# A two-layer encoder trunk: group A's attention in paired matmuls, an early activation table, the norm inside the MLP's squares, and another order of projections

## The chip, the core and the metric

The kernel runs on one core of one Trainium2 chip. The time is device microseconds of one execution. TensorE multiplies (a weight load, then columns that stream past it), VectorE and ScalarE do elementwise work and empty PSUM, GpSimd does memsets and some DMA, SyncE issues DMA. Each engine takes its own instructions strictly in order and they meet through semaphores.

## The reference

`x` is 512 tokens by 1024 features, and there are two layers. In each:

```
xn = RMSNorm(x)
[A | B | C | gates] = xn @ W_in            # 7296 columns
A: 3 groups x 2 heads of 64: windowed softmax attention, dilations 1, 4, 16;
   the groups are weighted by their softmax denominators
B: 4 heads: difference of two softmax maps, per-head RMSNorm
C: 4 heads: retention, both directions; per-head RMSNorm, times silu(cg)
m  = sum_i sigmoid(gate_i) * (branch_i @ W_branch_i)      # i = A, B, C
x  = x + m @ W_o
x  = x + relu(RMSNorm(x) @ W_1)^2 @ W_2                    # 4096 wide
```

All of it is float32. The kernel splits each operand into a rounded high part and the remainder (`hi`, `lo`) and multiplies hi\*hi + hi\*lo + lo\*hi, three matmuls for one product.

## The kernel before

Tokens are ordered so that a query tile of 128 rows (four tiles, index `j`) holds one residue class modulo 4. For dilations 4 and 16 (groups g = 1, 2) a tile then attends to itself alone (the "diagonal" groups); for dilation 1 (g = 0) all tiles meet (the "dense" group).

The work is a list of chunks, `sequence` (L822), each one `gemm` (L287): for pairs of 128 input rows ("units") a weight block is fetched by SyncE (`raw`), split by ScalarE and VectorE (`whi`, `wlo`, L282 and L283) and multiplied into four PSUM banks `acc0` to `acc3`. After the last unit, `done` empties each bank. The chunks A, B and C ("waves") make q, k and v of a group or a head. G makes 512 gate columns, W an output product with a branch's weights times its gate, cg the silu gate of C, O the product with W_o, M1 and M2 the two halves of the MLP, a quarter at a time. A wave has 96 matmuls of 384 columns (C: of 512), G 96 of 512.

The attention itself runs beside the chunks as "side" threads: `thread_prep` (norm, rope, transposes into `qk`), `thread_a`, `thread_b`, `thread_c`. `build` (L1022) interleaves their steps with the chunk's, by a table of costs per engine; a chunk can say that it needs a flag (W of A needs all of A's outputs, `("y", l, 0)`), and side steps then go on alone. `emit` (L1054) at last puts all instructions into one queue per engine, with the same costs, earliest start first. So an edit that alters a cost moves instructions on every engine. Side work uses four PSUM banks (`ps`), 55 SBUF tiles of 2 KB a partition (`U`) and two `qk` tiles.

`qk` holds q, then k's high part and a third slot that pairs q's remainder with k, so that a score takes two matmuls (`score`, L524). In `prep` (L473) the lower copy into that slot is a DVE copy (L520). For A, `vh` and `vl` are 128 wide per head with 64 columns zeroed by GpSimd (L443), so that two heads add into one bank `ps_a_tail`.

In the MLP, `norm_spread` makes `rB2`, the squared inverse norm spread over partitions. M1's `done` takes relu and squares on ScalarE without it. M2's sums over the four quarters are kept in `part` and multiplied by `rB2` at the end (L973 to L997); in the last layer the final sums go out in halves of 256 columns by DMA from SyncE and ScalarE in turn.

Of the kernel before, what the change touches and what calls it, by code (L numbers as in the profile page):

```python
# [9 lines left out]
FT = mybir.dt.float32  # L10
# [102 lines left out]
class Trunk:  # L113
# [202 lines left out]
    def setup(self):  # L316
# [90 lines left out]

    def norm_stat(self, square=False):
# [9 lines left out]
        if square:  # L418
            self.tt(r, r, r, OP.mult)
        return r  # L420
# [10 lines left out]
    def wave_buffers(self, kind):  # L431
        w = {"kind": kind}
        w["qk"] = self.take(self.qp, 2, "qk", [P, 6, SEQ], FR, "qk")
        if kind == "B":
            vt = [(self.U((P, NJ, P), FR, "vh"), self.U((P, NJ, P), FR, "vl"))]
        else:
            vt = [(self.U((P, NJ, P), FR, "vh"), self.U((P, NJ, P), FR, "vl")) for _ in range(2)]
        if kind == "A":
            for h in range(2):
                o = 64 * (1 - h)  # L440
                for t in vt[h]:
                    z = t.bitcast(FT)[:, :, o:o + 64]
                    self.op("POOL", 0.3, [t], [], lambda z=z: self.nc.gpsimd.memset(z, 0.0))  # L443
        w["v"] = vt
        w["t"] = [None, None]
        return w

    def wave_evac(self, w, j, bank):
        r = self.r[:, j:j + 1]
        if j % 2 == 0:  # L450
            w["t"][j // 2] = self.U((P, 2, 256), name="t")
        self.act(w["t"][j // 2][:, j % 2, :], bank[:, 0:256], AF.Copy, scale=r)
        for h, (vh, vl) in enumerate(w["v"]):
            if w["kind"] == "A":
                src, dst = bank[:, 256 + 64 * h:320 + 64 * h], slice(64 * h, 64 * h + 64)
            else:
                src, dst = bank[:, 256 + 128 * h:384 + 128 * h], slice(0, 128)
            self.act(vh[:, j, dst], src, AF.Copy, scale=r)
            self.stt(vl[:, j, dst], src, r, vh.bitcast(FT)[:, j, dst], OP.mult, OP.subtract)

# [12 lines left out]
    def prep(self, w, jp):  # L473
# [89 lines left out]

    def dense_out(self, w, vt, ws, av, first, last):
        for jk in range(NJ):
            hi, lo = self.to_keys(ws, jk)
            yield ("wait", "av")
            self.av_all(av, vt, jk, hi, lo, first and jk == 0, last and jk == NJ - 1)
            yield
# [59 lines left out]
    def b_tail(self, l, w, st):  # L629
        av = self.ps(name="ps_b_tail")  # L630
        yield from self.dense_out(w, w["v"][0], st["w"], av, True, True)
# [31 lines left out]
    def a_diag_scores(self, w, m, st, nmx, den, mask):  # L663
        ps = self.ps(name="ps_a_diag_scores")
        for j in range(NJ):
            self.score(w, (m,), j, (ps[:, j * P:(j + 1) * P],), n=P)
        sm = self.U(name="sm")
        s3 = sm.rearrange("p (j k) -> p j k", k=P)
        self.tt(s3, ps.rearrange("p (j k) -> p j k", k=P), mask[:, None, :].to_broadcast([P, NJ, P]), OP.add)
# [8 lines left out]
    def a_diag_out(self, w, m, st, av):  # L678
# [3 lines left out]
        hi, lo = self.split(b, "wT")  # L682
        yield ("wait", "dav")
        vh, vl = w["v"][m]
        for j in range(NJ):
            js = slice(j * P, (j + 1) * P)
            self.mm3(av[:, js], vh[:, j, :], vl[:, j, :], hi[:, js], lo[:, js], m == 0 and j == 0, m == 1 and j == NJ - 1)
        yield
# [52 lines left out]
    def a_tail(self, l, w, m, g, st, ys):  # L741
        if m == 0:
            w["av"] = self.ps(name="ps_a_tail")
        av = w["av"]
        if g == 0:
            yield from self.dense_out(w, w["v"][m], st, av, m == 0, m == 1)
        else:
            yield from self.a_diag_out(w, m, st, av)
        if m == 1:
            y = self.U(name="ya")  # L750
            self.act(y, av)
            ys.append(y)
            self.flags.add(("done", l, "A", g))
            yield

    def decay_table(self, l, h):
        T = self.take(self.Tp, 2, "T", [P, 896], FT, "T")
        dl = self.blob[:, C_DL - P:C_U - P]
        i = l * 4 + h
        self.act(T, dl, AF.Copy, scale=self.edec[:, 0, i:i + 1])  # L760
        self.stt(T, dl, self.edec[:, 1, i:i + 1], T, OP.mult, OP.min)
        self.act(T, T, AF.Exp)
        self.ts(T, T, 0.125)
        self.stt(T[:, 384:512], self.ident, 0.125, T[:, 384:512], OP.mult, OP.add)
        return T

    def c_head(self, l, w, m, h):
# [5 lines left out]
        for jk in range(NJ):  # L773
# [26 lines left out]
    def thread_prep(self, l):  # L800
        first = True
        for s in self.sequence:
# [12 lines left out]
            for jp in range(2):  # L815
# [5 lines left out]

    sequence = ([("A", 0), ("A", 1), ("A", 2), ("C", 0), ("C", 1), ("B", 0), ("B", 1), ("B", 2), ("cg",), ("G", 0, 0),  # L822
                 ("W", 0, 0), ("G", 0, 1), ("W", 0, 1), ("G", 2, 0), ("B", 3), ("W", 2, 0), ("G", 2, 1), ("W", 2, 1),
                 ("G", 1, 0), ("G", 1, 1), ("W", 1, 0), ("W", 1, 1), ("O", 0), ("O", 1)]
                + [x for i in range(4) for x in
# [24 lines left out]
    def layer(self, l, xg):  # L850
# [8 lines left out]
        h = [None] * 8  # L859
        part = {}  # L860
        self.side.append([self.thread_prep(l), None])
# [3 lines left out]
        for s in self.sequence:  # L865
# [84 lines left out]
            elif kind == "M1":  # L950
                def done(o, b):
                    t = self.U(name="rl")
                    self.act(t, b, AF.Relu)
                    hi = self.U(dt=FR, name="hh")
# [6 lines left out]
                if s[1] == 0:  # L961
                    def stat():
                        self.r2 = self.norm_stat(square=True)

# [4 lines left out]
            elif kind == "M2":  # L969
# [3 lines left out]
                def done(o, b):  # L973
                    k = s[2] * 4 + o
                    x = self.xt[k]
                    if s[1] == 0:
                        t = self.U(name="part")
                        self.act(t, b)
                        part[k] = t
                    elif s[1] < 3:  # L980
                        self.tt(part[k], part[k], b, OP.add)
                        if s[1] == 2:
                            t = part.pop(k)
                            self.tt(t, t, self.rB2, OP.mult)
                            self.tt(x, x, t, OP.add)
                    else:
                        t = self.U(name="fin")
                        self.xt[k] = None
                        for cs in ((slice(0, 256), slice(256, 512)) if last else (slice(0, 512),)):
                            self.tt(t[:, cs], b[:, cs], self.rB2[:, cs], OP.mult)  # L990
                            self.tt(x[:, cs], x[:, cs], t[:, cs], OP.add)
                            if last:
                                eng = self.nc.sync if o % 2 else self.nc.scalar
                                self.dma(eng, self.outv[k][:, cs], x[:, cs], 128, outs=[f"out{k}{cs.start}"])
                        if not last:
                            self.dma(self.nc.gpsimd, self.xspill[l + 1][k], x, 256, outs=[f"spill{l + 1}{k}"])
                            self.norm_feed(k, x)  # L997
                yield from self.gemm(c, h, done, False)
# [210 lines left out]
```

## Time and profile before

| | |
|---|---|
| runs (3) | median 1735.99 us, 1735.95 to 1737.02 |
| the profiled execution | 1736.39 us, its span 1733.8 us, granted clock 1.00 |
| TensorE busy | 1721.4 us (99%), 8232 matmuls |
| VectorE busy | 1084.2 us (63%) |
| ScalarE busy | 825.8 us (48%) |

The span is the time from the first to the last instruction of that execution. Busy matmul time is modelled at the ends, since matmuls overlap: a 512-column matmul is shown with 0.39 us, but the next one starts 0.227 us after it. What a matmul costs is therefore read from the starts of a run of them.

### The profile page before, as it was taken

The numbers are of one execution on the slowest core, as the hardware profiler recorded it, in microseconds if no ns is written. First come the engines' busy times: TensorE is split into PE (matmuls) and PEld (weight loads), VectorE is DVE, ScalarE is ACT, GpSimd is POOL, SyncE is SP. The second block draws the span as 40 slices with busy tenths as digits, with TensorE's granted clock in tenths as the row PEclk, the third lists the DMA queues.
The fourth block names the chain that finished last, engine by engine and source line by source line (L and its number), as shares of the span: only waits on it lengthen the run. The fifth ranks groups of instructions, "written<-read, shape, count | busy, mean of one in ns | idle before, by whom it ended". The sixth has DMA issues, their size and how long they took to land.

```text
span 1733.8 us, 21771 instructions
## 1 busy us (share of the span) xinstructions
PE 1721.4 (99%) x8232; PEld 1467.4 (85%) x8232; DVE 1084.2 (63%) x2123; ACT 825.8 (48%) x1514; POOL 19.5 (1%) x52
## 2 busy tenths in 40 slices
PE   8999999999999999999999999999999999999998
PEld 8889888888888888888898898888888888888887
DVE  8788998786554233344577889987766532333534
ACT  7567655554334342424456666546433453515151
POOL 0000000001000000000100000000000000000000
PEclk9999999999999999999999999999999999999999
DMA  6212222223222222222332112212232223232222
GB/s 219 100 46 71 74 67 81 72 98 122 98 97 98 97 96 95 97 97 94 107 122 80 55 62 86 73 67 92 85 122 98 98 85 110 85 110 85 98 98 73
DMA packets 48969, 160.65 MB, mean 93 GB/s; under 512 B 5728, under 2 KB 8160, under 8 KB 48736
## 3 DMA queue, kind: packets, MB, share of 16 engines
q1 hardware_dynamic: 45504, 151.84, 25.4%
q0 software_dynamic: 1920, 6.29, 1.1%
q8 instruction: 64, 1.05, 0.2%
q10 hardware_dynamic: 1440, 1.13, 0.2%
q14 instruction: 41, 0.34, 0.1%
HBM read 155.05 MB, written 4.19 MB: 92 GB/s over the span
## 4 chain that ended last, share of the span: by engine, by line
PE 97%; DVE 2%; ACT 1%; issue 0%; DMA 0%; DVEq 0%; ACTq 0%
PE acc L224 86%; PE ps_c_head L224 2%; PE ps_b_scores L224 2%; PE ps_b_tail L224 1%; PE ps_a_tail L224 1%; PE ps_to_keys L228 1%; PE ps_prep L228 1%; PE ps_a_dense_scores L224 0%; PE ps_a_diag_scores L224 0%; PE ps_yb L228 0%; PE ps_yt L228 0%; DVE wlo L185 0%; ACT vh L175 0%; ACT whi L175 0%; PE ps_a_diag_out L228 0%
## 5 line engine op out<-in xcount | busy, mean ns | idle before, releaser
L185 DVE TENSOR_TENSOR wlo<-raw,whi 128x1024 fp32r<-128x1024 f32 (+3 forms) x297 | 344.8, 1162 | 455.2 <-ACT whi L175 454.1
L175 ACT ACTIVATE whi<-raw 128x1024 fp32r<-128x1024 f32 (+3 forms) x297 | 299.9, 1010 | 631.2 <-PE acc L224 555.4
L224 PE MATMUL acc<-xgh,whi 128*128 128x512 f32 x960 | 376.5, 392 | 0.0
L224 PE MATMUL acc<-xgl,whi 128*128 128x512 f32 x960 | 374.1, 390 | 0.0
L224 PE MATMUL acc<-xgh,wlo 128*128 128x512 f32 x960 | 373.8, 390 | 0.0
L224 PEld LDWEIGHTS acc<-xgh,wlo 128*128 128x128 f32 x960 | 180.2, 188 | 37.8
L224 PEld LDWEIGHTS acc<-xgl,whi 128*128 128x128 f32 x960 | 180.3, 188 | 36.7
L224 PEld LDWEIGHTS acc<-xgh,whi 128*128 128x128 f32 x960 | 180.3, 188 | 36.7
L224 PE MATMUL acc<-whi,xgh 128*128 128x384 f32 (+1 forms) x576 | 202.4, 355 | 6.8 <-ACT whi L175 6.6
L224 PE MATMUL acc<-wlo,xgh 128*128 128x384 f32 (+1 forms) x576 | 201.2, 349 | 0.0
L224 PE MATMUL acc<-whi,xgl 128*128 128x384 f32 (+1 forms) x576 | 201.1, 349 | 0.0
L224 PE MATMUL acc<-hh,whi 128*128 128x512 f32 x512 | 199.2, 389 | 0.0
L224 PE MATMUL acc<-hl,whi 128*128 128x512 f32 x512 | 199.2, 389 | 0.0
L224 PE MATMUL acc<-hh,wlo 128*128 128x512 f32 x512 | 199.2, 389 | 0.0
L224 PEld LDWEIGHTS acc<-whi,xgh 128*128 128x128 f32 x576 | 108.4, 189 | 14.9 <-ACT whi L175 6.9
L224 PEld LDWEIGHTS acc<-wlo,xgh 128*128 128x128 f32 x576 | 108.9, 189 | 6.2 <-DVE wlo L185 0.3
L224 PEld LDWEIGHTS acc<-whi,xgl 128*128 128x128 f32 x576 | 108.6, 189 | 5.3
L224 PEld LDWEIGHTS acc<-hl,whi 128*128 128x128 f32 x512 | 96.1, 188 | 20.0
L224 PEld LDWEIGHTS acc<-hh,wlo 128*128 128x128 f32 x512 | 96.1, 188 | 19.9
L224 PEld LDWEIGHTS acc<-hh,whi 128*128 128x128 f32 x512 | 96.1, 188 | 19.9
L175 ACT ACTIVATE qk<-ps_prep 64x512 fp32r<-64x512 f32 (+1 forms) x144 | 69.9, 486 | 45.3 <-PE ps_prep L228 23.0
L185 DVE TENSOR_TENSOR hl<-rl,hh 128x512 fp32r<-128x512 f32 x64 | 44.4, 693 | 74.4 <-ACT rl L175 74.4
(202 smaller groups left out, 2285.3 us busy)
## 6 DMA issues: line engine op xcount, KB each, us to landing
raw<-in_weights_dram SPq DMA_DIRECT2D x236, 512.0 KB, 3.2
raw<-in_weights_dram SPq DMA_DIRECT2D x55, 384.0 KB, 3.0
xt<-in_x_dram SPq DMA_DIRECT2D x8, 256.0 KB, 5.8
xr<-in_x_dram POOLq DMA_DIRECT2D x8, 256.0 KB, 4.1
xspill<-xr POOLq DMA_DIRECT2D x8, 256.0 KB, 2.3
xr<-xspill POOLq DMA_DIRECT2D x8, 256.0 KB, 4.1
blob<-in_blob_dram SPq DMA_DIRECT2D x1, 1024.0 KB, 8.5
raw<-in_weights_dram SPq DMA_DIRECT2D x4, 256.0 KB, 2.6
```

What stands on the lines that cost most here:

```text
L175: lambda: self.nc.scalar.activation(out, in_, func, **k))
L185: self.dve(out, [out], [a, b], lambda: self.nc.vector.tensor_tensor(out, a, b, op=op))
L224: self.op("PE", d, [out], [lhsT, rhs], lambda: self.nc.tensor.matmul(out, lhsT, rhs, start=start, stop=stop))
L228: self.op("PE", 0.095, [out], [in_], lambda: self.nc.tensor.transpose(out, in_, ident))
```

## The change

- Group A's `v` is one tile per head: 64 columns high part, 64 columns remainder, side by side. One matmul gives both products with a given right side, in the upper and lower 64 partitions, which are then added. The GpSimd zeroing goes. Each head and, in the diagonal groups, each pair of query tiles has its own PSUM bank; ScalarE copies the upper half and VectorE adds.
- In the diagonal groups, scores and output products take both right sides (high and low) in one matmul of 256 columns instead of two or three of 128.
- A one-element `Exp` of a zeroed tile is issued at the start, so ScalarE's table load stands ahead of the first wait for data.
- `rB2` is no longer squared; M1's `done` computes max(b, 0) \* rB on VectorE and then squares. M2 adds its four quarters straight into `x`. In the last layer only the last column block goes out in halves.
- The low copy in `prep` moves from VectorE to ScalarE. In C the factor 0.125 moves from the decay table (a VectorE pass of 896 columns) into the product with the scores.
- `sequence`: G and W of branch A are put among the B waves, and cg after B2.

```diff
@@ setup
+        warm = cp.tile([P, 2], FT, name="warm")
+        self.op("POOL", 0.1, [warm], [], lambda: nc.gpsimd.memset(warm, 0.0))
+        self.act(warm[:, 1:2], warm[:, 0:1], AF.Exp)
         self.dma(nc.scalar, self.gcol, a["cols"], 18)
...
@@ wave_evac
+        if w["kind"] == "A":
+            for h, v in enumerate(w["v"]):
+                src = bank[:, 256 + 64 * h:320 + 64 * h]
+                self.act(v[:, j, 0:64], src, AF.Copy, scale=r)
+                self.stt(v[:, j, 64:128], src, r, v.bitcast(FT)[:, j, 0:64], OP.mult, OP.subtract)
+            return
...
@@ prep
-            self.copy(qk[own[m], 4 + m, qs], qk.bitcast(FT)[own[1 - m], 2 + m, qs])
+            self.act(qk[own[m], 4 + m, qs], qk.bitcast(FT)[own[1 - m], 2 + m, qs])
...
@@ dense_out
+                self.mm(av, vt[:, jk, :], hi, jk == 0, False)
+                self.mm(av, vt[:, jk, :], lo, False, jk == NJ - 1)
...
@@ a_diag_scores
-        ps = self.ps(name="ps_a_diag_scores")
-        for j in range(NJ):
-            self.score(w, (m,), j, (ps[:, j * P:(j + 1) * P],), n=P)
+        for p in range(2):
+            ps = self.ps((P, 2, 2, P), name="ps_a_diag_scores")
+            for j in range(2):
+                js = slice((2 * p + j) * P, (2 * p + j + 1) * P)
+                self.mm(ps[:, j], qk[:, m, js], qk[:, 2 + m:5 + m:2, js], j == 0, j == 1)
+            half = s3[:, 2 * p:2 * p + 2]
+            self.tt(half, ps[:, :, 0, :], mask[:, None, :].to_broadcast([P, 2, P]), OP.add)
+            self.tt(half, half, ps[:, :, 1, :], OP.add)
...
@@ a_diag_out
-            self.mm3(av[:, js], vh[:, j, :], vl[:, j, :], hi[:, js], lo[:, js], m == 0 and j == 0, m == 1 and j == NJ - 1)
+            av = self.ps((P, 2, 2, P), name="ps_a_tail")
+            for j in range(2):
+                self.mm(av[:, j], w["v"][m][:, 2 * p + j, :], ws[p][:, j], j == 0, j == 1)
+            t = self.U(name="yl")
+            t3 = t[0:64, 0:256].rearrange("p (j q) -> p j q", q=P)
+            self.act(t3, av[64:128, :, 0, :])
+            self.tt(t3, t3, av[0:64, :, 0, :], OP.add)
+            self.tt(y[own, 256 * p:256 * p + 256].rearrange("p (j q) -> p j q", q=P), t3, av[0:64, :, 1, :], OP.add)
...
@@ a_tail (dense group)
+            self.act(t[0:64], av[64:128])
+            self.tt(y[64 * m:64 * m + 64], t[0:64], av[0:64], OP.add)
...
@@ decay_table, c_head
-        self.ts(T, T, 0.125)
-            self.tt(t, ps, T[:, (3 - jk) * P:(7 - jk) * P], OP.mult)
+            self.stt(t, ps, 0.125, T[:, (3 - jk) * P:(7 - jk) * P], OP.mult, OP.mult)
...
@@ sequence
-    ("A", 0), ("A", 1), ("A", 2), ("C", 0), ("C", 1), ("B", 0), ("B", 1), ("B", 2), ("cg",), ("G", 0, 0), ("W", 0, 0), ...
+    ("A", 0), ("A", 1), ("A", 2), ("C", 0), ("C", 1), ("G", 0, 0), ("B", 0), ("B", 1), ("W", 0, 0), ("B", 2), ("G", 0, 1), ("cg",), ("W", 0, 1), ...
...
@@ M1 done
-                    self.act(t, b, AF.Relu)
+                    self.stt(t, b, 0.0, self.rB2, OP.max, OP.mult)
...
@@ M2 done
+                    if s[1] < 3:
+                        self.tt(x, x, b, OP.add)
+                        return
+                    ends = last and s[2] == 1 and o == NJ - 1
+                    for cs in ((slice(0, 256), slice(256, 512)) if ends else (slice(0, 512),)):
+                        self.tt(x[:, cs], x[:, cs], b[:, cs], OP.add)
```

The places in the queues of which the prediction speaks, where names carry the number of their buffer. First TensorE in layer 0, where a diagonal group's output product for one head (`ps_a_tail`) stands among a chunk's matmuls. Before, its first rows, the three of them coming four times:

```order
L224 MATMUL acc_340<-whi_345,xgl_140 128x512
L224 MATMUL ps_a_tail_353<-wTh_355,vh_158 128x128
L224 MATMUL ps_a_tail_353<-wTl_356,vh_158 128x128
L224 MATMUL ps_a_tail_353<-wTh_355,vl_159 128x128
L224 MATMUL ps_a_tail_353<-wTh_355,vh_158 128x128
```

and now, with the same kind of head whole:

```order
L224 MATMUL acc_364<-xgh_111,wlo_348 128x512
L224 MATMUL ps_a_tail_372<-wT_355,v_157 128x256 x2
L224 MATMUL ps_a_tail_374<-wT_356,v_157 128x256 x2
L224 MATMUL acc_365<-xgh_107,whi_347 128x512
L224 MATMUL acc_365<-xgl_108,whi_347 128x512
```

Twelve matmuls of 128 columns have become four of 256, and the chunk around them is now a gate chunk (`xgh` on the left) instead of a wave.

Second, the start of ScalarE's queue (`xt` a tile of x, `gcol` the gains, `xgh` its high part, `raw` the first weights). Before:

```order
L234 DMA gcol<-in_cols_dram 128x36
L234 DMA eye<-in_blob_dram 128x128
L175 ACT_TABLE_LOAD
L175 ACTIVATE xgh_108<-xt_86,gcol 128x512
L175 ACTIVATE sq_132<-xt_86 128x512
L175 ACTIVATE whi_106<-raw_87 128x384
```

and now:

```order
L234 DMA gcol<-in_cols_dram 128x36
L234 DMA eye<-in_blob_dram 128x128
L175 ACT_TABLE_LOAD
L175 ACTIVATE warm<-warm 128x1
L175 ACTIVATE xgh_107<-xt_87,gcol 128x512
L175 ACTIVATE sq_131<-xt_87 128x512
L175 ACTIVATE whi_105<-raw_88 128x384
```

The load stands in the same place in the queue, but before it waited for the first tile of x on behalf of the instruction behind it, and now it belongs to `warm` and waits for nothing.

Third, the end of VectorE's queue (`xr` a tile of x, `fin` the product with rB). Before:

```order
L185 TENSOR_TENSOR fin_2937<-acc_2929,rB_2595 128x256
L185 TENSOR_TENSOR fin_2938<-acc_2930,rB_2595 128x256
L185 TENSOR_TENSOR xr_2543<-xr_2543,fin_2938 128x256
L185 TENSOR_TENSOR xr_2541<-xr_2541,fin_2936 128x256
L185 TENSOR_TENSOR fin_2938<-acc_2930,rB_2595 128x256
L185 TENSOR_TENSOR xr_2542<-xr_2542,fin_2937 128x256
L185 TENSOR_TENSOR xr_2543<-xr_2543,fin_2938 128x256
```

and now:

```order
L185 TENSOR_TENSOR wlo_2937<-raw_2927,whi_2936 128x1024
L185 TENSOR_TENSOR xr_2555<-xr_2555,acc_2930 128x512
L185 TENSOR_TENSOR xr_2556<-xr_2556,acc_2931 128x512
L185 TENSOR_TENSOR xr_2557<-xr_2557,acc_2932 128x512
L185 TENSOR_TENSOR xr_2558<-xr_2558,acc_2933 128x256 x2
```

Behind the last bank (`acc_2930` before, `acc_2933` now) six instructions stood, two of them of earlier column blocks; now two stand there.

## Rows read from the trace of the kernel before

**Rows 1.** The page's busy times by engine

```profile
PE 1721.4 (99%) x8232; PEld 1467.4 (85%) x8232; DVE 1084.2 (63%) x2123; ACT 825.8 (48%) x1514; POOL 19.5 (1%) x52
```

**Rows 2.** The waits of TensorE (line waited for: us in total, times, longest)

```profile
PE acc L224 <- ACT whi L175: 6.6, 1, 6.6
```

**Rows 3.** Groups of group A's matmuls by form (count | busy us, modelled mean ns | idle)

```profile
L224 PE MATMUL ps_a_tail<-wTh,vh 128*128 128x512 f32 x16 | 6.4, 402 | 0.0
L224 PE MATMUL ps_a_tail<-wTh,vh 128*128 128x128 f32 x32 | 8.4, 264 | 0.0
L224 PE MATMUL ps_a_diag_scores<-qk 128*128 128x128 f32 x64 | 8.4, 274 | 0.3 <-DVE wTl L185 0.3
```

**Rows 4.** TensorE's timeline (start us, us), first and last of three runs of matmuls

```profile
38.14 0.33 PE L224 MATMUL acc<-wlo,xgh 128*128 128x384 f32 x1
...
40.74 0.33 PE L224 MATMUL acc<-wlo,xgh 128*128 128x384 f32 x1
...
120.98 0.28 PE L224 MATMUL ps_a_tail<-wTl,vh 128*128 128x128 f32 x1
...
122.10 0.28 PE L224 MATMUL ps_a_tail<-wTh,vl 128*128 128x128 f32 x1
...
505.19 0.39 PE L224 MATMUL acc<-mh,whi 128*128 128x512 f32 x1
...
511.99 0.39 PE L224 MATMUL acc<-mh,whi 128*128 128x512 f32 x1
```

**Rows 5.** The timeline's end, last matmul and VectorE's last work

```profile
1728.16 0.39 PE L224 MATMUL acc<-hh,wlo 128*128 128x512 f32 x1
...
1728.23 0.78 DVE L185 TENSOR_TENSOR fin<-acc,rB 128x256 f32<-128x256 f32 x2
...
1730.06 0.75 DVE L185 TENSOR_TENSOR xr<-xr,fin 128x256 f32<-128x256 f32 x2
```

**Rows 6.** The timeline's start

```profile
3.60 1.28 ACT L175 ACT_TABLE_LOAD   x1 [3.60 <-DMA xt<-in_x_dram]
...
4.90 0.72 ACT L175 ACTIVATE xgh<-xt,gcol 128x512 fp32r<-128x512 f32 x1
...
5.29 0.71 SPq L234 DMA_DIRECT2D raw<-in_weights_dram  x1
...
6.60 1.65 PE L224 MATMUL acc<-whi,xgh 128*128 128x384 f32 x4 [6.60 <-ACT whi L175]
...
25.55 0.96 DVE L185 TENSOR_TENSOR wlo<-raw,whi 128x768 fp32r<-128x768 f32 x1
...
26.57 0.44 PE L224 MATMUL acc<-wlo,xgh 128*128 128x384 f32 x1
```

**Rows 7.** Busy us by window, TensorE, weight loads, VectorE, ScalarE, GpSimd; clock, DMA

```profile
86.70:130.00 43.30, 43.30 (x246) 36.99 (x246) 38.24 (x85) 29.41 (x74) 0.00 (x0) 1.00 0.15 47
130.00:173.40 43.40, 43.40 (x266) 42.07 (x266) 38.72 (x76) 30.92 (x68) 0.00 (x0) 1.00 0.21 70
563.90:850.00 286.10, 286.10 (x1264) 236.97 (x1263) 109.66 (x121) 109.04 (x144) 2.46 (x7) 1.00 0.28 97
```

**Rows 8.** Costs on VectorE (count | busy us, mean ns | idle)

```profile
L185 DVE TENSOR_TENSOR fin<-acc,rB 128x256 f32<-128x256 f32 x16 | 6.4, 419 | 10.4 <-PE acc L224 10.1
L219 DVE CAST qk<-qk 64x256 fp32r<-64x256 f32 x72 | 20.8, 289 | 2.1
L189 DVE TENSOR_SCALAR T<-T 128x896 f32<-128x896 f32 x8 | 5.0, 622 | 0.0
```

**Rows 9.** The timeline where the MLP of layer 0 begins

```profile
537.22 0.58 ACT L175 ACTIVATE rB<-ps_norm 128x512 f32<-128x512 f32 x1
...
538.31 0.60 ACT L175 ACTIVATE rl<-acc 128x512 f32<-128x512 f32 x1 [0.51 <-PE acc L224]
```

**Rows 10.** Group A's last output bank emptied, and its last remainder made

```profile
141.08 0.60 ACT L175 ACTIVATE ya<-ps_a_tail 128x512 f32<-128x512 f32 x1
...
150.34 0.69 DVE L185 TENSOR_TENSOR ynl<-ya,ynh 128x512 fp32r<-128x512 f32 x1
```

More of the change, by code (lines that the diff above doesn't have):

```diff
@@ L433, in wave_buffers @@
         w["qk"] = self.take(self.qp, 2, "qk", [P, 6, SEQ], FR, "qk")
-        if kind == "B":
-            vt = [(self.U((P, NJ, P), FR, "vh"), self.U((P, NJ, P), FR, "vl"))]
-        else:
[L437 to L443, printed above, removed]
+        if kind == "A":
+            vt = [self.U((P, NJ, P), FR, "v") for _ in range(2)]
+        else:
+            vt = [(self.U((P, NJ, P), FR, "vh"), self.U((P, NJ, P), FR, "vl")) for _ in range(1 + (kind == "C"))]
         w["v"] = vt
@@ L452, in wave_evac @@
         self.act(w["t"][j // 2][:, j % 2, :], bank[:, 0:256], AF.Copy, scale=r)
-        for h, (vh, vl) in enumerate(w["v"]):
[L454 to L459, printed above, removed]
+        if w["kind"] == "A":
[4 more added lines that the diff above has]
+            return
+        for h, (vh, vl) in enumerate(w["v"]):
+            src = bank[:, 256 + 128 * h:384 + 128 * h]
+            self.act(vh[:, j], src, AF.Copy, scale=r)
+            self.stt(vl[:, j], src, r, vh.bitcast(FT)[:, j], OP.mult, OP.subtract)
     def prep_stats(self, w):
@@ L562, in b_scores, with dense_out @@
             yield ("wait", "key") if j == NJ - 1 else None
-    def dense_out(self, w, vt, ws, av, first, last):
+    def dense_out(self, vt, ws, av):
         for jk in range(NJ):
@@ L567, in dense_out @@
             yield ("wait", "av")
-            self.av_all(av, vt, jk, hi, lo, first and jk == 0, last and jk == NJ - 1)
+            if isinstance(vt, tuple):
+                self.av_all(av, vt, jk, hi, lo, jk == 0, jk == NJ - 1)
+            else:
+                self.mm(av, vt[:, jk, :], hi, jk == 0, False)
+                self.mm(av, vt[:, jk, :], lo, False, jk == NJ - 1)
             yield
@@ L630, in b_tail @@
         av = self.ps(name="ps_b_tail")
-        yield from self.dense_out(w, w["v"][0], st["w"], av, True, True)
+        yield from self.dense_out(w["v"][0], st["w"], av)
         st["w"] = None
@@ L663, in a_diag_scores @@
     def a_diag_scores(self, w, m, st, nmx, den, mask):
[L664 to L666 removed]
+        qk = w["qk"]
         sm = self.U(name="sm")
         s3 = sm.rearrange("p (j k) -> p j k", k=P)
[L669 removed]
+        for p in range(2):
[6 more added lines that the diff above has]
+            self.tt(half, half, ps[:, :, 1, :], OP.add)
         self.rmax(nmx[:, m * 4:m * 4 + 4], s3)
@@ L681, in a_diag_out @@
             self.tr(b[:, j * P:(j + 1) * P], st[0][:, j * P:(j + 1) * P], self.ident)
-        hi, lo = self.split(b, "wT")
-        yield ("wait", "dav")
-        vh, vl = w["v"][m]
-        for j in range(NJ):
-            js = slice(j * P, (j + 1) * P)
-            self.mm3(av[:, js], vh[:, j, :], vl[:, j, :], hi[:, js], lo[:, js], m == 0 and j == 0, m == 1 and j == NJ - 1)
+        ws = []
+        for p in range(2):
+            src = b[:, 256 * p:256 * p + 256].rearrange("p (j q) -> p j q", q=P)
+            t = self.U((P, 2, 2, P), FR, "wT")
+            self.act(t[:, :, 0, :], src)
+            self.tt(t[:, :, 1, :], src, t.bitcast(FT)[:, :, 0, :], OP.subtract)
+            ws.append(t)
+        yield ("wait", "dav")
+        own = slice(64 * m, 64 * m + 64)
+        for p in range(2):
+            av = self.ps((P, 2, 2, P), name="ps_a_tail")
[6 more added lines that the diff above has]
+            self.tt(y[own, 256 * p:256 * p + 256].rearrange("p (j q) -> p j q", q=P), t3, av[0:64, :, 1, :], OP.add)
         yield
@@ L742, in a_tail @@
         if m == 0:
-            w["av"] = self.ps(name="ps_a_tail")
-        av = w["av"]
+            ys.append(self.U(name="ya"))
+        y = ys[g]
         if g == 0:
-            yield from self.dense_out(w, w["v"][m], st, av, m == 0, m == 1)
+            av = self.ps(name="ps_a_tail")
+            yield from self.dense_out(w["v"][m], st, av)
+            t = self.U(name="yl")
+            self.act(t[0:64], av[64:128])
+            self.tt(y[64 * m:64 * m + 64], t[0:64], av[0:64], OP.add)
         else:
-            yield from self.a_diag_out(w, m, st, av)
+            yield from self.a_diag_out(w, m, st, y)
         if m == 1:
-            y = self.U(name="ya")
-            self.act(y, av)
-            ys.append(y)
             self.flags.add(("done", l, "A", g))
@@ L975, in done @@
                     x = self.xt[k]
[L976 to L997, printed above, removed]
+                    if s[1] < 3:
+                        self.tt(x, x, b, OP.add)
+                        return
+                    self.xt[k] = None
+                    ends = last and s[2] == 1 and o == NJ - 1
+                    for cs in ((slice(0, 256), slice(256, 512)) if ends else (slice(0, 512),)):
+                        self.tt(x[:, cs], x[:, cs], b[:, cs], OP.add)
+                        if last:
+                            eng = self.nc.sync if o % 2 else self.nc.scalar
+                            self.dma(eng, self.outv[k][:, cs], x[:, cs], 128, outs=[f"out{k}{cs.start}"])
+                    if not last:
+                        self.dma(self.nc.gpsimd, self.xspill[l + 1][k], x, 256, outs=[f"spill{l + 1}{k}"])
+                        self.norm_feed(k, x)
                 yield from self.gemm(c, h, done, False)
```

15 lines of the change are left out of this document (5 added, 10 removed), and 3 rows, old and new, of the table sequence.

## The prediction

> **What bounds the kernel now.** I read the page's busy times first [rows 1]: TensorE is busy 1721.4 of 1733.8 us, and a modelled busy time could hide waits inside it. So the second view is who TensorE waited for [rows 2]: one wait of 6.6 us for the first weights, and nothing else of weight. The third is its timeline [rows 4], since only the starts tell what a matmul costs. Thirty matmuls of 512 columns start between 505.19 and 511.99, 0.227 us each; fifteen of 384 columns between 38.14 and 40.74, 0.173 each; ten of 128 columns between 120.98 and 122.10, 0.112 each. The span is then three pieces: 6.60 us before the first matmul [rows 6], 1721.95 us to the end of the last one at 1728.55, and 5.27 us behind it [rows 5]. The middle piece is TensorE's own work, so the time is the work taken from TensorE, plus what the ends give, less new waits.
>
> **The change, part by part.** Group A on TensorE. The counts before are 48 matmuls of 512 columns (16 of each of three products), 96 of 128 columns in the diagonal output products (32 of each) and 64 of 128 columns in the diagonal scores [rows 3]. The dense group keeps two of three: 16 fewer at 0.227, 3.6 us off. The diagonal groups give up 160 of 128 columns at 0.112, 17.9 us, and get 64 of 256 columns (32 for scores, 32 for outputs). The trace has no matmul of 256 columns. It can't cost less than one of 128 (0.112, so 7.2 us) and not more than one of 384 (0.173, so 11.1 us). I take the line through 384 and 512 columns: 0.173 less 0.053 for 128 columns is 0.120, 7.7 us. Together 3.6 + 17.9 - 7.7 = 13.8 us come off, between 10.4 and 14.3. Transposes and all other matmuls keep their number.
>
> The Trainium skill has a rule that speaks against this. "TensorE: Matmul & The Clock Gate", section "Wait — 56ns, not 53.3ns?", gives the start-to-start time of a warm matmul as its columns over 2.4 GHz plus about 2.5 ns, 55.6 ns at 128 columns and 215.7 at 512, for bf16. By that two of 128 columns cost as much as one of 256, and joining them gives nothing. This trace has 112 ns and 227 ns; at 128 columns it is twice the rule, so the rule does not hold for these short matmuls, and the row decides. What would be left if time went by columns alone is a rival below.
>
> The end. The last matmul ends at 1728.55; VectorE still has a pair of halves from 1728.23, more behind them, and finishes the last pair (1730.06, 0.75) at 1730.81, and the output goes out behind that [rows 5]. Now only two half additions stand behind the last bank: a pair takes 0.75 to 0.78, so 1728.6 + 0.8 = 1729.4, and 1.4 us come off. It can be worth nothing, if one of the larger transfers of the other column blocks should now land last, and not more than 1.5.
>
> The start. The table load of 1.28 us ran from 3.60, after the first tile of x had landed, and the first ScalarE product followed at 4.90 [rows 6]. With the load ahead of that wait, this product can start at about 3.7, 1.2 earlier. The first weights had landed by 5.29, where SyncE's entry behind them is issued, so their split ends at about 5.8 and TensorE starts 0.75 us earlier than 6.60. But that lead isn't kept: the matmul at 26.57 starts as VectorE's `wlo` of 25.55 ends, and VectorE's instructions up to there are the same, in the same order, without idle time from the second tile of x on. I take 0.3, between 0 and 1.2.
>
> VectorE and ScalarE. In the stretch where A, C and the first B waves run, VectorE is busy 38.24 and 38.72 of 43.3 us [rows 7], so what is added to it counts. In each layer group A adds 16 half-width mask and sum passes at 0.42 [rows 8] in place of 4 of 0.69 (4.0 us), 8 halves of a remainder in place of 4 whole ones (0.6), and 16 halves and 2 whole additions for the outputs (8.1): 12.7 us. Off go 36 casts at 0.289 (10.4 us) and 4 table passes at 0.622 (2.5) [rows 8]. So over a layer it is even, but A's share comes early and the casts are spread over nine waves. What covers it is the gate chunk that now stands behind C1: 96 matmuls at 0.227 give 21.8 us of TensorE, for about 8 us of VectorE. The casts become ScalarE work, 36 a layer at 0.3 to 0.6 (bounds: VectorE's own price, and ScalarE's for 512 columns [rows 10]), on an engine with 12 us free in each of these windows. I price all this at nothing but for small waits in the new order, where VectorE is still the tightest: 1.5 us in all, between -2 (some waits of before vanish) and 8.
>
> The MLP. Per layer VectorE gets 32 products for ScalarE's 32 relus, and loses 16 passes in M2: 11 us net on an engine that is busy 110 of 286 us there [rows 7], all beside matmuls. The one new wait: M1's first bank can't be emptied before `rB` is there. It is started at 537.22, and the first bank was emptied at 538.31 [rows 9], so it is just in time; and if it were late, the bank is wanted again only after 18 matmuls of the other three, 4.1 us. Nothing.
>
> The moved output product. W of branch A needs A's outputs. From its last bank (141.08) to its last remainder (150.34 + 0.69) 10 us go by [rows 10]; in the new order all of B1, 96 matmuls at 0.173, 16.6 us, stands between. Nothing. GpSimd's zeroing was on no path.
>
> The sum against the profiled execution: 1736.39 - 13.8 - 1.4 - 0.3 + 1.5 = 1722.4. It is 0.4 above the median of the runs, 1735.99, so the forecast for a median is 1722.0.
>
> **Rivals.** *Columns alone count.* Two matmuls of 128 columns cost what one of 256 does. For: the rule above, and that no row shows a 256. Against: 384 columns cost only 1.5 times what 128 do. At 0.224 for a 256 the new ones take 14.3 us, TensorE gives 3.6 + 17.9 - 14.3 = 7.2, and the time is 1728.6.
>
> *VectorE becomes the bound where A's sums come in, and it gets slower.* For: 77 of 86.7 us are already busy there [rows 7], and the queue is strict, so a split of weights (`wlo`) behind A's sums holds TensorE. Price: if TensorE waits for all of the added 12.7 us in each layer, 25.4 us come on and the sum is 1747.4. It decides when VectorE's load passes TensorE's time in that stretch: 77 + 12.7 - 4.6 (four waves' casts) + 8 = 93 us, against 86.7 + 21.8 - 6.9 = 101.6 of matmuls. Some 8 us are still free, so this takes that I mis-size A's sums by two thirds. A part of it, waits of 4 to 9 us in places, is likelier: 1725 to 1731.
>
> *The early table load does nothing and the end little.* Then 1.7 us stay: 1723.7, inside the range.
>
> **How the numbers follow.** The forecast as worked out, 0.72; columns alone, 0.08; waits of 4 to 9 us, 0.13; the slower case 0.04 and something in between that comes out even 0.03. The best of all bounds (14.3, 1.5, 1.2 and two us of waits gone) is 1717.0 against the median; the range goes from there to 1729, which takes in columns alone and most of the partial waits. A run of this kernel can tell 0.2%, 3.5 us: faster means under 1732.5. That holds in the first three cases, 0.92 after a little is taken off; even 0.04; slower 0.04.
>
> **What will show it.** Runs of `ps_a_tail` and `ps_a_diag_scores` with starts 0.12 apart (0.22 would make the first rival right); TensorE busy down by about 13.8 us; one wait of some 5.9 us at the start and a repeat of the wait at 26; VectorE's last addition ending 0.8 after the last matmul; no wait of TensorE for `wlo`, `yl` or `ya` between 90 and 200 us worth over a us. The prediction is wrong if TensorE's list of waits gets a second entry of several us, or if the span falls by under 8 us.

## The result and the profile after

| | before | changed |
|---|---|---|
| median of the runs (range) | 1735.97 (1735.82 to 1737.02) | 1721.42 (1720.98 to 1722.02) |
| profiled execution | 1736.39 | 1721.42 |
| its span | 1733.8 | 1719.6 |
| first matmul starts | 6.60 | 5.48 |
| matmuls at their undisturbed spacing | 1711.1 | 1697.3 |
| spacing beyond that | 10.4 | 12.9 |
| from the last matmul's start to the end | 5.67 | 4.00 |

The ratio is 0.9915 (0.9903 to 0.9928): 14.6 us faster, 0.6 us beside the forecast. The lower four rows add up to each span. The undisturbed spacing is, for both kernels, 0.1735 us for each of 1344 matmuls of 384 columns, 0.2267 for 512 columns (6176 before, 6160 after), 0.109 for each of 552 transposes, 0.112 for the 160 of 128 columns that only the kernel before has, and 0.120 for the 64 of 256 columns that only the changed one has. What is left of the time from the first matmul's start to the last's is the "spacing beyond that" ("beyond" from here on): waits, short delays, and stretches at the lower clock.

The page's busy times [rows 1] and TensorE's waits [rows 2] are now these (line waited for: us in total, times, longest):

```profile
PE 1709.5 (99%) x8120; PEld 1454.8 (85%) x8120; DVE 1094.3 (64%) x2126; ACT 813.0 (47%) x1529; POOL 13.3 (1%) x29
```

```profile
PE acc L224 <- ACT whi L175: 5.5, 1, 5.5
PE acc L224 <- DVE v L194: 0.5, 1, 0.5
PE ps_c_head L224 <- ACT wTh L175: 0.3, 1, 0.3
```

There are 112 matmuls fewer and two small waits more; the wait for the first weights is 1.1 shorter. Group A's matmuls [rows 3] by form, and one run of four in the timeline [rows 4] (start us, us):

```profile
L224 PE MATMUL ps_a_tail<-wTl,v 128*128 128x512 f32 x16 | 6.6, 412 | 0.0
L224 PE MATMUL ps_a_tail<-wTh,v 128*128 128x512 f32 x16 | 6.6, 412 | 0.0
L224 PE MATMUL ps_a_tail<-wT,v 128*128 128x256 f32 x32 | 5.5, 283 | 0.0
L224 PE MATMUL ps_a_diag_scores<-qk 128*128 128x256 f32 x32 | 5.1, 282 | 0.0
```

```profile
154.29 0.64 PE L224 MATMUL ps_a_tail<-wT,v 128*128 128x256 f32 x4
```

The 0.64 us of four, less the 0.28 of the last, is three spacings of 0.12. The mean of 283 ns is a modelled duration and no cost, as it was before. The end [rows 5] and the start [rows 6], in the timeline:

```profile
1.66 1.28 ACT L175 ACT_TABLE_LOAD   x1 [1.66 <-PEq L1207]
...
3.77 0.72 ACT L175 ACTIVATE xgh<-xt,gcol 128x512 fp32r<-128x512 f32 x1 [0.61 <-DMA gcol<-in_cols_dram]
...
11.08 0.38 PE L224 MATMUL acc<-whi,xgl 128*128 128x384 f32 x1
11.30 0.33 PE L224 MATMUL acc<-whi,xgh 128*128 128x384 f32 x1
...
24.83 0.60 PE L228 MATMUL ps_norm<-eye,sq 128*128 128x128 f32 x4
25.51 0.96 DVE L185 TENSOR_TENSOR wlo<-raw,whi 128x768 fp32r<-128x768 f32 x1
...
1715.65 0.39 PE L224 MATMUL acc<-hh,wlo 128*128 128x512 f32 x1
1716.07 0.75 DVE L185 TENSOR_TENSOR xr<-xr,acc 128x256 f32<-128x256 f32 x2 [0.67 <-PE acc L224]
```

The last addition ends at 1716.82, 0.8 us behind the last matmul (1716.04), where it was 2.3. At the start ScalarE's first product of x (`xgh`) begins 1.13 us earlier, and by 25.5 the lead over the trace of before is 0.04. The windows [rows 7], with one of 101.6 us more, which is the stretch that the prediction counted (busy us of TensorE, weight loads, VectorE, ScalarE, GpSimd; clock, DMA):

```profile
86.70:130.00 43.30, 43.30 (x222) 35.77 (x221) 35.17 (x68) 31.36 (x77) 0.00 (x0) 1.00 0.19 62
130.00:173.40 43.40, 43.40 (x252) 41.21 (x251) 35.09 (x78) 28.09 (x67) 0.00 (x0) 1.00 0.23 73
86.70:188.30 101.60, 101.60 (x549) 90.59 (x548) 82.12 (x165) 69.34 (x166) 0.00 (x0) 1.00 0.21 67
```

VectorE is busy 82 of 101.6 us there, less than the 93 that the prediction put down.

### The profile page after: what moved, and what is told of

Same layout as the page of the kernel before. It is cut to its first block, busy times and chain, and to the rows that moved or that the text cites. A ratio compares the mean times of both kernels' runs of the same rounds, so it can differ in the third digit from the quotient of the medians.

```text
span 1719.6 us, 21537 instructions
## 1 busy us (share of the span) xinstructions
PE 1709.5 (99%) x8120; PEld 1454.8 (85%) x8120; DVE 1094.3 (64%) x2126; ACT 813.0 (47%) x1529; POOL 13.3 (1%) x29
## 3 DMA queue, kind: packets, MB, share of 16 engines
q10 hardware_dynamic: 864, 1.13, 0.2%
## 5 line engine op out<-in xcount | busy, mean ns | idle before, releaser
L185 DVE TENSOR_TENSOR wlo<-raw,whi 128x1024 fp32r<-128x1024 f32 (+2 forms) x297 | 345.0, 1162 | 456.7 <-ACT whi L175 456.0
L175 ACT ACTIVATE whi<-raw 128x1024 fp32r<-128x1024 f32 (+2 forms) x297 | 300.2, 1011 | 629.8 <-PE acc L224 560.7
L185 DVE TENSOR_TENSOR xr<-xr,acc 128x512 f32<-128x512 f32 (+1 forms) x81 | 54.6, 678 | 30.6 <-PE acc L224 30.1
```

The source lines that it names most:

```text
L175: lambda: self.nc.scalar.activation(out, in_, func, **k))
L185: self.dve(out, [out], [a, b], lambda: self.nc.vector.tensor_tensor(out, a, b, op=op))
```

## Experiments

Three parts can be told apart: **A** (group A's buffers, scores and outputs), **order** (the new `sequence`), and the **rest** (early table load, the MLP, the cheaper decay table, the low copies on ScalarE). All eight combinations ran. "Beyond" is as in the table above; medians of before in these runs are 1736.1 to 1736.7.

| parts | median | ratio (95%) | beyond | TensorE's waits beside the first weights |
|---|---|---|---|---|
| none (before) | 1736.2 | 1 | 10.4 | none |
| A | 1734.98 | 0.9991 (0.9982 to 0.9999) | 23.3 | `sd` 5.5, `ynh` 1.2 |
| order | 1742.13 | 1.0030 (1.0018 to 1.0041) | 17.1 | `yn` 2.4, `gate` 0.7 |
| rest | 1733.62 | 0.9984 (0.9975 to 0.9993) | 11.1 | `vl` 1.0 |
| A + order | 1731.98 | 0.9974 (0.9964 to 0.9985) | 20.7 | `y` 2.0, `gate` 1.9, `yn` 1.1 |
| A + rest | 1726.57 | 0.9949 (0.9936 to 0.9963) | 17.7 | `gate` 2.2, `u` 2.2 |
| order + rest | 1740.35 | 1.0025 (1.0016 to 1.0034) | 17.4 | `gate` 1.9, `yn` 2.3, `vl` 1.3 |
| all (changed) | 1721.42 | 0.9915 (0.9903 to 0.9928) | 12.9 | `v` 0.5, `wTh` 0.3 |

In these lists `sd` is C's scores times the decay table, `y` a head's output, `yn` and `ynh` its normalized form and that one's high part, `v` and `vl` remainders of v, `wTh` the high part of the transposed weights of the attention, `u` a step of `prep`.

The list of waits holds only a part of "beyond", and not all of the rest is short delays. In the traces of A, of the order, and of A + order TensorE's granted clock falls to 0.50 (the 1.2 GHz level) once in the middle, behind a wait, and the matmuls of 512 columns there start 0.43 us apart instead of 0.227: 1.7, 1.7 and 1.5 us of "beyond". The first 50 us, which none of the three parts but the early load touches, hold 2.8 to 4.0 in those traces and in that of before, since the clock also rises at another time in each. So a difference of one or two us between two numbers of this column can't be put down to a part.

**A alone.** The kernel before with the new group A.

```diff
...
-        vh, vl = w["v"][m]
...
-            self.mm3(av[:, js], vh[:, j, :], vl[:, j, :], hi[:, js], lo[:, js], ...)
...
+                self.mm(av[:, j], w["v"][m][:, 2 * p + j, :], ws[p][:, j], j == 0, j == 1)
```

> The kernel before with group A's part of the change alone (v side by side, 256-column matmuls, a bank per pair), in the old order of the chunks. Theory (time is TensorE's work plus the two ends): 13.4 us less than before, 1722.6, TensorE's waits no longer than before. Rival (VectorE becomes the bound where A's 12.7 us a layer come in, and it is the gate chunk moved behind C1 that makes room): waits of 4 us and more between 80 and 200 us of the span, so 1727 or more, 1747 if all of it is waited for.

Measured 1734.98, as the rival has it: of the 13.9 us that TensorE is rid of, 12.9 come back as spacing beyond (23.3 against 10.4). About 1.0 of that lies in the first 50 us, in which A has no part. Its list of waits, its timeline at one of them, and its window:

```profile
PE ps_c_head L224 <- DVE sd L185: 5.5, 2, 2.8
PE acc L224 <- ACT ynh L175: 1.2, 2, 0.6
```

```profile
178.97 0.68 DVE L185 TENSOR_TENSOR u<-t,Cg 128x512 f32<-128x512 f32 x1
179.69 0.29 DVE L185 TENSOR_TENSOR u<-u,sm 128x128 f32<-128x128 f32 x1
180.02 0.69 DVE L185 TENSOR_TENSOR u<-u,rs 128x512 f32<-128x512 f32 x1
180.74 1.89 DVE L185 TENSOR_TENSOR sd<-ps_c_head,T 128x512 f32<-128x512 f32 x3
181.49 0.73 PE L224 MATMUL ps_c_head<-qk 128*128 128x512 f32 x2 [2.79 <-DVE sd L185]
```

```profile
86.70:188.30 101.60, 98.76 (x546) 88.89 (x545) 94.28 (x208) 69.77 (x164) 0.00 (x0) 0.98 0.19 56
```

VectorE is busy 94.3 of 101.6 us, and without a break at 179 to 182; the `sd` that empties a score bank stands behind a wave's normalization (`rs`, `u`), and TensorE waits for the bank. The 0.98 in the window's row is the clock: behind that wait, from 182.9 to 186.2, it is 0.50. The second layer has the like wait of 2.7 us (at 1040.92) with the clock at 1.00 behind it. So the list of waits of the kernel before, empty but for the start, did not say that work may be taken off TensorE for nothing.

**The new order alone.**

```diff
-... ("C", 1), ("B", 0), ("B", 1), ("B", 2), ("cg",), ("G", 0, 0), ("W", 0, 0), ...
+... ("C", 1), ("G", 0, 0), ("B", 0), ("B", 1), ("W", 0, 0), ("B", 2), ("G", 0, 1), ("cg",), ...
```

> The kernel before with the new sequence alone. Theory: TensorE had no waits to lose between 50 and 1700 us in the kernel before, so a new order has nothing to give: 1736 within 1 if it opens none, 1738 to 1742 if the gate chunks among the B waves wait for VectorE as they do with the old group A in the changed kernel (1740.4 there). Rival (the order is worth microseconds by itself, as the step from 1735.0 to 1732.0 with the new group A suggests): 1733 or less.

Measured 1742.13, at the slow end of the theory's figures; the rival is wrong. One wait in layer 0, TensorE's transposes behind a head norm, holds 2.4 of the 6 us, and the stretch behind it, at half the clock, 1.7 more:

```profile
298.13 0.67 PE L228 MATMUL ps_to_keys<-eye,e 128*128 128x128 f32 x4 [2.37 <-DVE yn L185]
```

```profile
298.60:302.00 3.40, 3.40 (x10) 2.69 (x9) 3.33 (x8) 0.60 (x1) 0.00 (x0) 0.50 0.00 0
```

This kernel's executions differ by that: two of the six, with a granted clock of 1.000 in the mean, took 1739.8, and four, at 0.998 or 0.999, took 1742.0 to 1742.4. So some 3.7 of the 6 us are there without such a stretch, and the rest comes with it.

**The rest alone.** The changed kernel with the old A and the old order.

```diff
...
-    sequence = ([("A", 0), ..., ("C", 1), ("G", 0, 0), ("B", 0), ...
+    sequence = ([("A", 0), ..., ("C", 1), ("B", 0), ("B", 1), ("B", 2), ("cg",), ...
```

> The changed kernel with the old group A and the old order; only the rest of the change stays (early table load, rB in the squares, M2 summed on x, low copies on ScalarE, table pass gone). Theory (before, TensorE had hardly a wait, so work taken off VectorE gives nothing; the end gives 1.7): 1736.6 - 1.7 = 1734.9, within 1 us. Rival (the rest is worth as much by itself as it was on top of A's part in the old order, 1735.0 to 1726.6): 1728.

Measured 1733.62, 2.6 less than before and 0.3 under the theory's range: the end and the start, nothing in between ("beyond" 11.1 against 10.4).

**A and order, without the rest.**

The edit against the changed kernel takes all of the rest back; one place of it:

```diff
...
-            self.act(qk[own[m], 4 + m, qs], ...)
+            self.copy(qk[own[m], 4 + m, qs], ...)
...
```

> The kernel before with group A's part and the new order of the chunks, nothing else (casts on VectorE, table pass, old MLP and old start and end stay). The run with A's part alone lost 11 of its 13.4 us to waits of TensorE for VectorE around C's heads, 120 to 185 us into each layer, where VectorE was busy 28 of 30 us. Theory (TensorE's saving turns into waits where VectorE is full, and the moved gate and output chunks give TensorE other work there): most of the 13.4 us now comes, 1736.6 - 13.4 + 0 to 3 = 1723 to 1726. Rival (it is the work taken off VectorE, casts and table pass, that makes the saving count): as with A's part alone, 1733 to 1735.

Measured 1731.98, between the theory and the rival and nearer the rival. The rest alone gives 2.6, and behind A and order it gives 10.6. A part of the 10.6 is the clock: all seven executions of A and order have a granted clock of 0.997 to 0.999 in the mean, and the four of the changed kernel have 1.000.

**All but the order.**

```diff
-... ("C", 1), ("G", 0, 0), ("B", 0), ("B", 1), ("W", 0, 0), ...
+... ("C", 1), ("B", 0), ("B", 1), ("B", 2), ("cg",), ("G", 0, 0), ("W", 0, 0), ...
```

> The changed kernel with the old order of the chunks; all else stays. Theory: the order gives nothing that TensorE waits for, 1721.4 within 1 us. Rival (the gate chunk behind C1 is the cover for A's new VectorE work): waits there, 1726 to 1747.

Measured 1726.57: the order that costs 6 us by itself gives 5.2 here. The rival's time came out, but not its place: TensorE waits for `u` and `gate` at 256 to 260 and 1113 to 1116, and in the stretch from 86.7 to 188.3 it is busy 101.3 of 101.6 us, with VectorE at 93.2.

**All but A.**

```diff
...
-        if kind == "A":
-            vt = [self.U((P, NJ, P), FR, "v") for _ in range(2)]
...
+            vt = [(self.U((P, NJ, P), FR, "vh"), self.U((P, NJ, P), FR, "vl")) for _ in range(2)]
```

> The changed kernel with the old group A (three products, zeroed halves, 128-column matmuls); all else of the change stays. Theory: TensorE's 13.4 us come back, the end and the start stay as changed: 1721.4 + 13.4 = 1734.8, 1 to 2 us under before. Rival (a good part of the gain is from the new order and from what was taken off VectorE): 1728 or less.

Measured 1740.35, and both expectations missed: A is worth 18.9 us in the full change, more than the 13.9 of its matmuls. Beside the old A the new order costs microseconds here too, as it does alone; why was not tried.

**The price of one of 256 columns.** The changed kernel, each such matmul as two of 128, on the same data.

```diff
-                self.mm(ps[:, j], qk[:, m, js], qk[:, 2 + m:5 + m:2, js], j == 0, j == 1)
+                for i in range(2):
+                    self.mm(ps[:, j, i, :], qk[:, m, js], qk[:, 2 + m + 2 * i, js], ...)
...
```

> The changed kernel with each 256-column matmul of the diagonal groups issued as two of 128 columns on the same operands and banks: 64 matmuls become 128, the columns are the same. Theory: a short matmul has a floor, 128 columns cost 0.112 and 256 cost 0.119, so 64 x (0.224 - 0.119) = 6.7 us come on, 1728.1. Rival (columns alone count): 1721.4 within 0.5 us.

Measured 1728.31, 6.9 more: 64 matmuls more at 0.108. Eight of them in its timeline, on the average (1.01 - 0.27) / 7 = 0.106 apart:

```profile
154.45 1.01 PE L224 MATMUL ps_a_tail<-wT,v 128*128 128x128 f32 x8
```

So 256 columns cost what 128 do, within about a hundredth of a us, and the rival "columns alone count" is refuted.

**The low copy back on VectorE.** The changed kernel with one line of before.

```diff
-            self.act(qk[own[m], 4 + m, qs], qk.bitcast(FT)[own[1 - m], 2 + m, qs])
+            self.copy(qk[own[m], 4 + m, qs], qk.bitcast(FT)[own[1 - m], 2 + m, qs])
```

> The changed kernel with the low copy of prep back on VectorE, 36 a layer at 0.289 us. Theory (with the gate chunk behind C1 VectorE has 5 to 10 us in 30 free between 120 and 180 us): 0 to 2 us on, 1721.4 to 1723.4. Rival (VectorE is the bound in that stretch, and each us on it shows): 10 us a layer, in part or whole, 1727 to 1741.

Measured 1726.91, 5.5 more than with all of the change and just under the rival's range. Its waits, and the place of two of them in layer 0 (`yn` and the other `gate` are in layer 1); the profiled execution is one of 1729.3, with the clock at 0.50 behind the waits in both layers:

```profile
PE ps_b_scores L224 <- ACT y L175: 2.0, 1, 2.0
PE acc L224 <- DVE gate L194: 1.9, 2, 1.0
PE ps_yt L228 <- DVE yn L185: 1.1, 1, 1.1
```

```profile
279.63 1.47 PE L228 MATMUL ps_yt<-eye,y 128*128 128x128 f32 x12
285.08 0.60 PE L228 MATMUL ps_yt<-eye,y 128*128 128x128 f32 x4
287.72 0.70 PE L224 MATMUL ps_b_scores<-qk 128*128 128x512 f32 x2 [2.05 <-ACT y L175]
289.36 0.50 PE L224 MATMUL acc<-xgh,whi 128*128 128x512 f32 x1 [0.94 <-DVE gate L194]
```

Four head norms (four transposes each) are issued within 6 us; in the changed kernel it is three at 281.79 and the fourth at 296.77. `emit` places instructions by its engines' costs, so a dearer VectorE also moves the transposes. That left two causes: VectorE's added work, or the place of the norms.

**The same with the norms spread.** One number more, in the table by which `build` delays side steps (here the transposes of a head's output), on top of the copy on VectorE; every engine has the same instructions as with the copy alone.

```diff
-W = {"prep": 4.0, "y": 0.0, ...
+W = {"prep": 4.0, "y": 4.0, ...
...
```

> The changed kernel with the low copy of the preparation back on VectorE (1726.9 when run so), and one number of the planner's table raised, the delay after which the transposes of a head's output may be issued, 0 to 4: the same instructions on every engine, but the three head norms near 280 us no longer stand one behind the other in TensorE's order. Theory A (the 5.5 us are placement: three norms queued together in ScalarE's and VectorE's order): 1721.5 to 1723.5 and the waits of ps_b_scores for y gone. Theory B (the 5.5 us are VectorE's amount of work, 0.29 us more for each copy): still 1726 to 1728.

Measured 1722.97 (0.9922, 0.9909 to 0.9936): 3.9 of the 5.5 us are gone and so is the wait for `y`. In its timeline the norms now stand two, one and one:

```profile
279.16 1.07 PE L224 MATMUL ps_b_scores<-qk 128*128 128x512 f32 x4
282.36 1.04 PE L228 MATMUL ps_yt<-eye,y 128*128 128x128 f32 x8
288.24 0.60 PE L228 MATMUL ps_yt<-eye,y 128*128 128x128 f32 x4
295.53 0.60 PE L228 MATMUL ps_yt<-eye,y 128*128 128x128 f32 x4
```

So with the same work on VectorE another placement avoids most of that loss. The spread was not tried without the copy, so what the added work itself costs is not known; TensorE's list still has 1.7 for `vl` and 1.4 for `gate`.

**Without the early table load.**

```diff
...
-        self.act(warm[:, 1:2], warm[:, 0:1], AF.Exp)
```

> The changed kernel without the early load of the function table; nothing else differs. Theory (TensorE's clock takes the lead away): the first matmul starts 1.1 us later, but ps_norm again starts within 0.3 us of the 24.83 it has in the changed kernel, because fewer matmuls run at the 0.32 us spacing; time 1721.4 within 0.5. Rival (the lead is kept to the end): 1721.4 + 1.1 = 1722.5, and ps_norm a microsecond later.

Measured 1722.21, 0.8 more, and a span of 1720.1, 0.5 more: between the two figures, nearer the rival in time and the theory in `ps_norm`. Its first matmul is 1.25 later, `ps_norm` 0.40 later:

```profile
6.73 1.65 PE L224 MATMUL acc<-whi,xgh 128*128 128x384 f32 x4 [6.73 <-ACT whi L175]
...
10.67 0.51 PE L224 MATMUL acc<-whi,xgh 128*128 128x384 f32 x2
...
25.23 0.60 PE L228 MATMUL ps_norm<-eye,sq 128*128 128x128 f32 x4
```

Between these two traces a third of the lead is kept. The rest goes because matmuls start 0.32 us apart (384 columns at the 1.2 GHz level) for 3.9 us here, and in the changed kernel from 5.48 to 11.30, 5.8 us, before they go to 0.174. That this stretch was the longer one in the changed kernel's trace is chance, as the last section shows.

**Work for TensorE ahead of the first weights.** The changed kernel with nine matmuls on a zeroed tile.

```diff
...
+        for i in range(9):
+            self.mm(wb, wz[:, 0:P], wz, i == 0, i == 8)
```

> The changed kernel with nine matmuls of 512 columns on a zeroed tile at the very start, into a bank that nobody reads, while TensorE would wait for the first weights. The changed kernel's first matmul came 1.13 us earlier than before, but 17 of its matmuls ran 0.32 us apart instead of 11, and 24 us into the span it was level with before. Theory (the lead was lost to TensorE's lower clock): the first real matmuls now run 0.174 apart, and the first chunk ends 1 us or more earlier, so 1720.4 or less. Rival (VectorE's and ScalarE's splits of weights set that stretch anyway): the first chunk ends where it did, 1721.4.

Measured 1720.72 (1720.70 to 1722.13; ratio 0.9912, 0.9898 to 0.9925), 0.3 above what the theory asks for and the lowest median of all, though 0.7 us is less than a comparison of these runs can tell. The trace tells more:

```profile
1.35 4.21 PE L224 MATMUL ps_warm<-wz 128*128 128x512 f32 x9 [1.35 <-POOL wz L327]
5.45 1.65 PE L224 MATMUL acc<-whi,xgh 128*128 128x384 f32 x4
...
7.16 0.34 PE L224 MATMUL acc<-whi,xgl 128*128 128x384 f32 x1
...
23.25 0.60 PE L228 MATMUL ps_norm<-eye,sq 128*128 128x128 f32 x4
23.95 0.95 DVE L185 TENSOR_TENSOR wlo<-raw,whi 128x768 fp32r<-128x768 f32 x1
```

With the same first real matmul the slow spacing ends at 7.16, `ps_norm` starts 1.6 us earlier, and VectorE's `wlo` with it. Against all eight traces with the early load and nothing ahead, where `ps_norm` starts at 23.72 to 24.92, it is 0.5 to 1.7 earlier.

**The old MLP.** The changed kernel with the MLP of before.

```diff
...
+                            self.tt(t[:, cs], b[:, cs], self.rB2[:, cs], OP.mult)
+                            self.tt(x[:, cs], x[:, cs], t[:, cs], OP.add)
...
-                        self.tt(x[:, cs], x[:, cs], b[:, cs], OP.add)
```

> The changed kernel with the MLP of before: rB squared and applied where the second layer's sums leave PSUM, partial sums in an own tile. Theory: only the tail comes back, two VectorE passes where one stands now, on a whole or half tile: +1.4 to +1.7, so 1722.8 to 1723.2, and no wait of TensorE inside the MLP. Rival 1: the old MLP's ScalarE and VectorE work brings waits, 1725 or more. Rival 2: the tail is hidden, 1721.4.

Measured 1722.80, 1.4 more, with "beyond" at 13.2: the tail alone. Its last matmul starts at 1715.83 and VectorE's last pair only at 1717.73:

```profile
1715.83 0.39 PE L224 MATMUL acc<-hh,wlo 128*128 128x512 f32 x1
...
1717.73 0.75 DVE L185 TENSOR_TENSOR xr<-xr,fin 128x256 f32<-128x256 f32 x2
```

## Why the prediction was right

**TensorE, -13.8.** Measured -13.9 in the undisturbed spacings, with the 6.9 of the matmuls of 256 columns confirmed by splitting them. TensorE's busy time, which the prediction named as a sign of it, fell by only 11.9 (1721.4 to 1709.5): it contains the short delays, which grew. The value on the line through 384 and 512 columns, 0.120, is what a 256 took (0.12). The Trainium skill's rule of columns over 2.4 GHz plus 2.5 ns ("TensorE: Matmul & The Clock Gate", section "Wait — 56ns, not 53.3ns?") would give, as an estimate, 109 ns for 256 columns, against the 0.12 here, and 56 ns for 128, half of the 0.106 to 0.112 of these runs.

**The end, -1.4.** Measured -1.67 from trace to trace, and 1.4 when the old MLP was put back.

**The start, -0.3.** Between the two profiled executions the net is -0.3 (first matmul 1.1 earlier, 0.8 more beyond in the first 50 us). The number is luck, and the reason given was wrong. VectorE's `wlo` did not hold the lead back: it starts 0.7 behind `ps_norm` in every trace, and when TensorE came earlier (the nine matmuls ahead), that `wlo` started 1.6 us earlier too. TensorE spent the lead at the low clock, but only in this pair of traces. The low level ends at another time in each execution: in the five traces without the early load `ps_norm` starts at 24.87 to 26.02, in the eight with it and nothing ahead at 23.72 to 24.92, and the middle ones are 25.77 and 24.22. The kernel before was the earliest of its five, the changed kernel the latest but one of its eight. So most of the lead is kept as a rule; in the time, leaving out the early load cost 0.5 to 0.8.

**New waits, +1.5, and VectorE.** Beyond the first 50 us the spacing grew by 1.7, so the size is right. It is right only for the whole change. The prediction let the rival of a full VectorE decide at 101.6 us of load, and took 93 as safe. A alone shows 94.3, and there TensorE waits 2.8 us at once: a bank is emptied late where several long items stand ahead of it in VectorE's queue, before the engine is full. In the changed kernel the load was 82. The order alone and A + order show where the 11 us between lie:

```profile
86.70:188.30 101.60, 101.60 (x567) 90.37 (x566) 80.66 (x166) 62.94 (x139) 0.00 (x0) 1.00 0.18 58
86.70:188.30 101.60, 101.60 (x552) 90.64 (x551) 85.89 (x181) 63.90 (x153) 0.00 (x0) 1.00 0.21 65
```

With the order alone VectorE has 80.7 there, where the prediction has 77 + 8; A adds 5.2 within this stretch and not 12.7, the rest takes off 3.8 and not 4.6. So the sum for VectorE was too high mainly in A's part. The partial form of the rival is what comes when a part is left out beside the new A: 7.3 to 12.9 us more beyond than before, against 2.5 for the whole change, with up to 1.7 of it at the low clock.

**The MLP and W, nothing.** "Beyond" is at most 0.1 in every 50 us from 450 to 850 in both kernels, and W brought no entry in the list of waits.

**Outside the span.** Execution less span is 2.57 in the profiled run of before and 1.78 here. Other runs of the kernel before have 1.73 to 2.96, so these 0.8 us are no effect of the change.

What is left open: whether the waits with A alone, with the order alone and without A can be placed away too, as with the copy; spreading the norms was tried only for that one. And which part of the rest makes A and the order pay was tried only for the copy and the early load.

## What to carry to other kernels

Where one engine is busy all the time and waits for nobody, a saving on it is cashed only as far as the engines behind it can follow: the list of waits of the kernel before, empty but for the start, does not show it. The load of the second engine in a stretch does not show it either:

```profile
230.00:260.00 30.00, 30.00 (x151) 25.02 (x150) 28.24 (x84) 16.82 (x52) 0.00 (x0) 1.00 0.23 71
260.00:300.00 40.00, 37.63 (x175) 31.03 (x174) 32.92 (x80) 22.85 (x63) 0.00 (x0) 0.98 0.23 73
```

In the kernel before VectorE was busy 28.2 of 30 us (0.94) and TensorE waited for nothing; with the order alone it was busy 32.9 of 40 us (0.82) and TensorE stood for 2.4. With A alone it was what stood in VectorE's queue ahead of the one instruction that TensorE needed.

Parts of a change don't add: A gave 1 to 2 us alone and 18.9 with the rest, and the order cost 4 to 6 alone and gave 5 with the rest, so judge a reordering together with what it is to cover. Where a program places the instructions by costs, an edit of one engine's cost moves other instructions too; compare their places before a loss is put down to the added work.

## What was not expected of the hardware

At the start matmuls of 384 columns ran 0.32 us apart, the 1.2 GHz level, for 3.4 us before the change, 5.8 after it and 3.9 without the early load. That looks as if an earlier first matmul only made the slow stretch longer, but the other traces show that its end is a matter of the execution. With the early load and nothing ahead (eight traces) the first matmul starts at 5.28 to 5.56, and the granted clock goes to 1.00 anywhere from 8.2 to 11.5; without it (five traces) the first starts at 6.55 to 6.73, and the clock goes up at 9.9 to 12.5. With nine matmuls on zeros from 1.35 on, it went up at 7.1, earlier than in any other trace, and the real ones ran slow for 1.7 us only; but that is one trace.

The granted clock also fell to 0.50 in the middle of some executions, each time behind a wait of TensorE: from 298.6 to 302.0 with the order alone, behind 2.4 us; at 182.8 with A alone, behind 2.8; at 1149.1 with A and the order, behind 2.05 and 0.93; and, with the copy back on VectorE, at 290.1 behind 2.05 and 0.94 and at 1146.8 behind 1.1 and 1.0. Matmuls of 512 columns then started 0.427 us apart, which adds about 1.6 us each time. Other waits of the same size had no such stretch behind them (2.7 us in the second layer of A alone), nor had every execution of the same kernel. So a wait of TensorE can cost more than it lasts, and part of a difference between two medians can be this.

A matmul of 128 columns took 0.106 to 0.112 us from start to start in runs of them and one of 256 took 0.12; each has its own weight load. The rows point to the load as what sets that floor, though it was not tested: in the run of eight at 154.45 the loads start 0.11 us apart throughout, each matmul but the first starts 0.06 behind the start of its load, and the second comes only 0.06 behind the first.
